# One transfer for the first input tile, norm-weight rows asked first, and a changed order of two vector operations at the beginning of the MLP

## The chip, the cores and the metric

The kernel runs on one core of one Trainium2 chip. Its metric is device time in microseconds (us), taken as the median of several runs. One execution was also profiled, instruction by instruction; all rows shown are from that execution. TensorE is called PE, VectorE DVE, ScalarE ACT, GpSimd POOL and SyncE SP, as in the profile. SP and ACT also issue DMA transfers, and so does POOL.

## The reference

The reference is a trunk of two layers over 512 tokens of width 1024, all in float32. Cut to what matters here, a layer is:

```python
def hybrid_layer(x, ...):
    h = rmsnorm(x, norm_mix)            # x * rsqrt(mean(x^2) + eps) * gain
    z = h @ w_in                        # 1024 -> 4360 columns
    ...                                 # windowed attention, mLSTM, two gates
    x = x + mixed @ w_out
    u = jax.nn.relu(rmsnorm(x, norm_ffn) @ w_ff1)   # 1024 -> 4096
    return x + (u * u) @ w_ff2                      # 4096 -> 1024
```

## The kernel before

**Split products.** Every matrix product is made with float32 precision from two reduced parts of each operand: `high` is the operand rounded to float32r, `low` is the rest. A product is three matmuls, high by high, high by low and low by high (`mm3`, whose matmuls all carry L47, the line of the helper that records the latest PE instruction; PE transposes carry L52). The two parts of an activation are made by `split` (L196, L197, or L199, L200 with a scale), those of a weight by L186, L187 in the mixer and L1268, L1269 in the MLP: ACT makes the high part, and DVE subtracts it to make the low part.

**The norm.** The normalised activations are not formed directly. `Norm.turn(k)` transposes the k-th 128 columns of x (four PE transposes, one per block of 128 tokens, into one PSUM bank) and splits them with the norm gain as a scale per partition; the factor per token is applied later. So a bank with transposed x is read by ACT (high) and then by DVE (low), and it is free for the next transposes when both have read it.

**The start.** x lies in four tiles of 256 tokens by 512 columns. The first 128 columns come by two transfers, 256 tokens each, one issued by SP and one by ACT (`load_x`, L375). ACT then issues `gain0` (L382), the first 128 norm weights as one number to each of 128 partitions, and `grow0` (L383), all norm weights of the mixers as 16 rows of 128. Then come the next 128 columns of x, again by SP and by ACT, and ACT loads its activation table (L387). SP alternates pieces of x with the weight chunks of the first four output blocks (L159). Meanwhile PE multiplies a matrix of ones into a bank called `idle`, transposes the first tile of x, and multiplies ones once more. `turn_first` makes the high part of the first tile in two halves with `gain0` as the scale (ACT, L315) and queues the low part (DVE, L319) behind the split of the first weight chunk (DVE, L171 and L173). The first group of four output blocks runs term by term for k = 0: high weight by high x in four blocks, then low weight by high x, then high weight by low x, four matmuls each. Between the first and the second term PE transposes `grow0` into a spare part of the bank `idle`, DVE copies the result to `gcol` (L134), from which all later gains are taken, and PE transposes x for k = 1.

**The beginning of the MLP.** The MLP uses a fast scheme with half-sized blocks, seven products in place of eight, which needs sums and differences of quarters of x. `turn_whole(k)` for k = 0 to 3 transposes a piece of x into one of the two auxiliary PSUM banks; ACT copies the second token half with the gain (L1366) into a tile called `one`; `norm.turn` splits the whole piece (ACT L199, then DVE L200); and DVE makes the difference of the token halves, with the gain, from the bank and `one` (L1368). The bank thus has four readers. It is called twice after the first half-product and twice after the second, so the third and fourth call reuse the banks of the first and second.

**What sets the order.** A planner lists the instructions of each engine before the run, from its own estimates of durations: of those that it takes to be ready it issues the one with the lowest rank. Inside a `high_priority` block the ranks count from zero at the head of the block, so the place in its block is an instruction's rank against those of other such blocks. `issue_after` forces an order on one engine without a wait. At run time each engine's own list is fixed and executed in order. DMA transfers of SP and ACT are counted on eight completion counters in turn; a ninth transfer waits until the first has landed.

Of the kernel before, what the change touches and what calls it, by code (L numbers as in the profile page):

```python
# [8 lines left out]
F32 = mybir.dt.float32  # L9
# [7 lines left out]
P = 128  # L17
T = 512
NB = T // P
D = 1024  # L20
KT = D // P
# [8 lines left out]
LN_EXP = "natural_log_exp_and_others"  # L30
# [3 lines left out]
def hybrid_kernel(ctx, tc, x, norm_mix, w_in, att_q_norm, att_k_norm, att_sinks, m_gate_bias,  # L34
                  m_head_norm, w_att_branch, w_m_branch, w_out, norm_ffn, w_ff1, w_ff2,
                  rope_cos, rope_sin, out):
    nc = tc.nc
    ve, sc, gp = nc.vector, nc.scalar, nc.gpsimd

    latest = [None]  # L40
# [14 lines left out]
    const = ctx.enter_context(tc.tile_pool(name="const", bufs=1))  # L55
    small = ctx.enter_context(tc.tile_pool(name="small", bufs=3))
# [5 lines left out]
    def nm(s):  # L62
        uid[0] += 1
        return f"{s}_{uid[0]}"
# [33 lines left out]
    def aux(shape=(P, T)):  # L98
        return now["paux"].tile(list(shape), F32, tag="aux", name=nm("aux"))
# [4 lines left out]
    def f32(ap):  # L104
        return ap.bitcast(F32)
# [7 lines left out]
    grow0 = const.tile([16, P], F32, name="grow0")  # L113
# [11 lines left out]
    grow = const.tile([24, P], F32, name="grow")  # L125
    gcol = const.tile([P, 40], F32, name="gcol")

    first_gains = []

    def gains(row, c0, gps=None):  # L130
        n = row.shape[0]
        gps = aux([P, n]) if gps is None else gps
        pe.transpose(gps, row, ident[:n, :n])
        return ve.tensor_copy(gcol[:, c0:c0 + n], gps)  # L134

    def g_mix(l, k):
        return gcol[:, 8 * l + k:8 * l + k + 1]
# [8 lines left out]
    chunks, asked, lead, first_rest = [0], [None], [None], []  # L146

    def chunk(src, behind=()):

        with tc.high_priority():  # L150
            raw = now["wraw"].tile([P, T], F32, tag="w", name=nm("w"))
            off = 0
            for s in src:
                n = s.shape[1]
                if first_loads:

                    n0 = {0: 0, 1: 2}.get(chunks[0], len(first_loads) - 1)
                    with tc.issue_after(first_loads[n0].ins):
                        first_weights.append(nc.sync.dma_start(raw[:, off:off + n], s))  # L159
                    chunks[0] += 1  # L160
                    if chunks[0] == 8:
                        first_loads.clear()
                else:
                    asked[0] = nc.sync.dma_start(raw[:, off:off + n], s)
                off += n
        with tc.high_priority(lead[0]):
            wh = now["wsp"].tile([P, T], F32R, tag="wh", name=nm("wh"))
            wl = now["wsp"].tile([P, T], F32R, tag="wl", name=nm("wl"))
            n = chunks[0] - 1 if first_loads else KT
            if n == 0 and first_rest:  # L170
                high = ve.tensor_copy(wh[:, :off], raw[:, :off])  # L171
                with tc.issue_after(high.ins):
                    low = ve.tensor_tensor(wl[:, :off], raw[:, :off], f32(wh[:, :off]), op=ALU.subtract)  # L173
                with tc.issue_after(low.ins):
                    first_rest.pop()()
                return wh, wl
            with ExitStack() as order:
                for i in behind:
                    order.enter_context(tc.issue_after(i.ins))
                if n == 1:  # L180
                    order.enter_context(tc.issue_after(first_gains[0].ins))
                if n < KT:

                    order.enter_context(tc.issue_after(norm0.hi[max(n - 1, 0)].ins))
                    order.enter_context(tc.issue_after(norm0.lo[max(n - 1, 0)].ins))
                sc.activation(wh[:, :off], raw[:, :off], AF.Copy)  # L186
                ve.tensor_tensor(wl[:, :off], raw[:, :off], f32(wh[:, :off]), op=ALU.subtract)  # L187
        return wh, wl
# [169 lines left out]

    junk = const.tile([P, T], BF16, name="junk")

    xtok = [[const.tile([P, 2, T], F32, name=f"x{t}_{j}") for j in range(2)] for t in range(2)]
    gain0 = small.tile([P, 1], F32, tag="gain0", name=nm("gain0"), bufs=1)
    norm = norm0 = Norm(lambda k: g_mix(0, k) if k else gain0)
    first_loads, first_weights = [], []

    def load_late(k):

        with tc.high_priority(), tc.issue_after(first_weights[-1].ins):
            for t in range(2):
                load_x(k, 2, t, nc.sync)  # L370

    def load_x(k, n, t, by):

        c = (k % 4) * P
        first_loads.append(by.dma_start(  # L375
            xtok[t][k // 4][:, :, c:c + n * P],
            x[0, 2 * t * P:2 * (t + 1) * P, k * P:(k + n) * P].rearrange("(i p) n -> p i n", p=P)))

    with tc.high_priority():
        load_x(0, 1, 0, nc.sync)  # L380
        load_x(0, 1, 1, nc.scalar)
        nc.scalar.dma_start(gain0, norm_mix[0, 0:P].rearrange("(p o) -> p o", o=1))  # L382
        nc.scalar.dma_start(grow0, norm_mix.rearrange("l (k p) -> (l k) p", p=P))  # L383
        load_x(1, 1, 0, nc.sync)
        load_x(1, 1, 1, nc.scalar)
        with tc.issue_after(first_loads[-1].ins):
            sc.preload_act_table_set(LN_EXP)  # L387
        for t in range(2):
            load_x(2, 2, t, nc.sync)

        idle = aux()
        for n in (2, 2, 2):
            pe.matmul(idle[:, :n * P], ones, ones.unsqueeze(1).to_broadcast([P, n, P]), start=True, stop=True)
        with tc.issue_after(latest[0].ins):
            x0 = [aux((P, 2 * P)) for _ in range(2)]
            for b in range(NB):
                pe.transpose(x0[b // 2][:, b % 2 * P:(b % 2 + 1) * P], xtok[b // 2][0][:, b % 2, 0:P], ident)
        with tc.issue_after(latest[0].ins):
            pe.matmul(idle[:, :P], ones, ones, start=True, stop=True)
        norm.turn_first(x0)  # L400
# [838 lines left out]
    def mlp(l, norm, phase):  # L1239
# [117 lines left out]
        def turn_whole(k):  # L1357

            ps = norm.transposes(k)
            if not whole:  # L1360
                whole[:] = [quads.tile([P, 4, H], F32, tag="q5", name=nm("x")),
                            uspl.tile([P, 4, H], F32, tag="uh", name=nm("x"))]
                scratch["b"] = quads.tile([P, 4, H], F32, tag="s", name=nm("x"))
            one = whole[k % 2][:, k, :]
            with tc.high_priority():
                sc.activation(one, ps[:, H:T], AF.Copy, scale=norm.gain(k))  # L1366
                norm.turn(k, ps)
                ve.scalar_tensor_tensor(scratch["b"][:, k, :], ps[:, :H], norm.gain(k), one,  # L1368
                                        op0=ALU.mult, op1=ALU.subtract)

        def x22():
            h22, l22 = [f32(a) for a in quad(1, 1)]
            scratch["a"] = uspl.tile([P, 4, H], F32, tag="ul", name=nm("x"))
            plus(scratch["a"], h22, l22)
# [402 lines left out]
        p = second_slots(0, us[0])  # L1777
        slots = [f0[2], f1[2], f0[1], f0[5], p[1], f0[6], f0[7], f0[4], f0[3],
                 f1[1], p[5], f1[5], p[6], f1[6], p[3], f1[7], p[7], f1[3], p[4], f1[4], p[2]]
        for part in range(1, 4):  # L1780
            p = second_slots(part, us[part])
            if part < 3:
                f = first_slots(part + 1, us[part + 1])[1]
# [34 lines left out]
        def squares():  # L1818
            with tc.issue_after(sums_made[3][0].ins):
                norm.squares(0)  # L1820

        turns = [(1.0 + k // 2, lambda k=k: turn_whole(k)) for k in range(4)]
        x22()
        weave([(1.0, go) for _, go in steps[:10]], turns + [(9.0, squares), (9.0, factor)])
# [8 lines left out]
    def turn_behind(norm, k):  # L1833

        with tc.issue_after(latest[0].ins):
            norm.turn(k)

    def gains_behind():

        with tc.issue_after(latest[0].ins):  # L1840
            first_gains.append(gains(grow0, 0, idle[:, 2 * P:2 * P + 16]))

    late = ([(0.2, gains_behind)] + [(max(0.25, k - 0.85), lambda k=k: turn_behind(norm, k)) for k in range(1, KT)]
            + [(3.0, lambda: load_late(4)), (4.0, lambda: load_late(6))]
            + [(6.5, late_gains)]
            + [(3.0 + 2.2 * j, lambda j=j: norm.squares(j)) for j in range(2)])
    order = None
    for l in range(DEPTH):
        with start if l == 0 else ExitStack() as phase:
            if l > 0:  # L1850
                psum_pools(phase, 3)
            norm = mixer(l, norm, late, order, phase)
        with ExitStack() as phase:
            psum_pools(phase, 2)
            norm = mlp(l, norm, phase)
        late = []
        if norm:
            late = [(0.75, lambda k=k, norm=norm: turn_behind(norm, 6 + k)) for k in range(2)]
            late += [(1.25, lambda norm=norm: norm.squares(1))]
            late += norm.steps(0, 1.75, 0.5, lambda k, norm=norm: turn_behind(norm, k))  # L1860
        order = [4, 5, 6, 7, 0, 1, 2, 3]
# [40 lines left out]
```

## Time and profile before

| | |
|---|---|
| median of 3 runs | 1261.53 us (1261.37 to 1263.22) |
| the profiled execution | 1262.1 us, of which the span is 1260.4 us |
| busy: PE, weight loads, DVE, ACT, POOL | 1254.8, 1100.6, 1029.8, 813.5, 281.1 us |
| first matmul of the program | starts 1.08 us into the span |
| first matmul on x | recorded from 5.73 us |
| transposes of the third `turn_whole` | start at 325.45 us (layer 0), 950.15 us (layer 1) |

The span is the time from the first to the last instruction; what lies around it, 1.7 us here, is launch and end. PE executes in order, and its matmuls overlap, so a row gives the start of the first and the time to the end of the last; the distance between the starts of neighbours is the cost of one. Idle time in brackets names what ended it.

### The profile page before, as it was taken

What the parts mean: (1) busy time and instruction counts of PE and PEld (TensorE: products, weight loads), DVE (VectorE), ACT (ScalarE), POOL (GpSimd) and SP (SyncE); (2) the same over time, 40 slices, a digit from 0 to 9 for tenths busy, and PEclk for the clock granted to TensorE, in tenths of its full rate; (3) what the DMA queues carried; (4) which work ended last, traced back from release to release, by engine and by line L of the source; (5) the groups of instructions that cost most, each with busy time, mean ns of one, the idle gap of its engine ahead of it and who ended that gap; (6) DMA issues with size and microseconds to landing.
All of it is one profiled execution on the core that took longest, in us unless ns stands there. A gap on an engine that the chain in (4) does not pass through costs nothing.

```text
span 1260.4 us, 19852 instructions
## 1 busy us (share of the span) xinstructions
PE 1254.8 (100%) x7178; PEld 1100.6 (87%) x7178; DVE 1029.8 (82%) x1598; ACT 813.5 (65%) x1443; POOL 281.1 (22%) x373
## 2 busy tenths in 40 slices
PE   9999999999999999999999999999999999999998
PEld 7888888888999899999888888888889999999987
DVE  4788997688998887878857989876889988778787
ACT  5578578646685665656554885876467766556563
POOL 4513231021222021131115032310303211311300
PEclk9999999999999999999999999999999999999999
DMA  5424573469799889997224354644778997998943
GB/s 164 118 70 128 134 129 97 130 140 236 156 250 181 234 171 212 234 188 199 35 76 118 88 130 118 118 117 117 157 219 178 239 199 220 172 227 203 200 134 101
DMA packets 145410, 199.68 MB, mean 158 GB/s; under 512 B 10904, under 2 KB 85504, under 8 KB 145312
## 3 DMA queue, kind: packets, MB, share of 16 engines
q0 software_dynamic: 50432, 68.30, 33.8%
q1 hardware_dynamic: 94016, 129.72, 33.1%
q8 instruction: 56, 0.92, 0.3%
q10 hardware_dynamic: 864, 0.40, 0.1%
q14 instruction: 42, 0.34, 0.1%
HBM read 195.24 MB, written 2.10 MB: 157 GB/s over the span
## 4 chain that ended last, share of the span: by engine, by line
PE 98%; DVE 1%; DMA 0%; issue 0%; ACTq 0%; ACT 0%; DVEq 0%
PE mm L47 83%; PE aux L47 12%; PE aux L52 2%; DVE wl L1269 1%; DMA gain<-in_norm_mix_dram 0%; DVE i L200 0%; DVE x L1314 0%; DVE raw L1314 0%; DVE x L1368 0%; ACTq L375 0%; DVE x L1333 0%; ACT i L315 0%; DVEq L200 0%; ACTq L315 0%
## 5 line engine op out<-in xcount | busy, mean ns | idle before, releaser
L1268 ACT ACTIVATE wh<-raw 128x1024 fp32r<-128x1024 f32 x224 | 234.8, 1054 | 152.1 <-PE mm L47 85.1
L1269 DVE TENSOR_TENSOR wl<-raw,wh 128x1024 fp32r<-128x1024 f32 x224 | 271.5, 1221 | 72.2 <-ACT wh L1268 69.4
L47 PE MATMUL mm<-i,wh 128*128 128x256 f32 (+1 forms) x1344 | 330.3, 338 | 0.0
L47 PEld LDWEIGHTS mm<-i,wh 128*128 128x128 f32 x1344 | 225.0, 190 | 20.5
L47 PE MATMUL mm<-i,wl 128*128 128x256 f32 (+1 forms) x672 | 224.4, 334 | 0.0
L47 PE MATMUL mm<-wh,uh 128*128 128x512 f32 (+1 forms) x444 | 173.1, 390 | 0.0
L47 PE MATMUL mm<-wl,uh 128*128 128x512 f32 (+1 forms) x444 | 172.8, 389 | 0.0
L47 PE MATMUL mm<-wh,ul 128*128 128x512 f32 (+1 forms) x444 | 172.3, 388 | 0.0
L1431 POOL DMA_DIRECT2D raw<-in_w_ff_dram x56 | 72.5, 1375 | 343.3 <-DVE wl L1269 91.4
L47 PEld LDWEIGHTS mm<-i,wl 128*128 128x128 f32 x672 | 127.6, 190 | 13.3
L187 DVE TENSOR_TENSOR wl<-w,wh 128x512 fp32r<-128x512 f32 (+1 forms) x143 | 94.4, 665 | 34.0 <-ACT wh L186 31.6
L186 ACT ACTIVATE wh<-w 128x512 fp32r<-128x512 f32 (+1 forms) x143 | 85.0, 601 | 54.4 <-PE mm L47 48.0
L47 PE MATMUL mm<-t,wh 128*128 128x256 f32 x576 | 104.5, 283 | 0.0
L47 PE MATMUL mm<-wh,i 128*128 128x512 f32 (+1 forms) x352 | 98.7, 357 | 0.4 <-ACT i L315 0.4
L47 PEld LDWEIGHTS mm<-wh,ul 128*128 128x128 f32 x444 | 83.4, 188 | 17.4
L47 PEld LDWEIGHTS mm<-wh,uh 128*128 128x128 f32 x444 | 83.5, 188 | 16.1
L47 PEld LDWEIGHTS mm<-wl,uh 128*128 128x128 f32 x444 | 83.5, 188 | 15.7
L47 PEld LDWEIGHTS mm<-t,wh 128*128 128x128 f32 x576 | 90.7, 192 | 1.3
L1683 POOL DMA_DIRECT2D raw<-in_w_ff_dram x40 | 48.2, 1207 | 175.9 <-DVE wl L1269 136.8
L1333 DVE SCALAR_TENSOR_TENSOR x<-mm,ms,x 128x512 f32<-128x512 f32 (+1 forms) x103 | 73.0, 743 | 11.3 <-PE mm L47 11.0
L47 PE MATMUL mm<-t,wl 128*128 128x256 f32 x288 | 81.5, 283 | 0.0
L47 PEld LDWEIGHTS mm<-wh,i 128*128 128x128 f32 x352 | 62.3, 189 | 9.6 <-ACT i L315 0.7
(333 smaller groups left out, 2517.3 us busy)
## 6 DMA issues: line engine op xcount, KB each, us to landing
raw<-in_w_ff_dram SPq DMA_DIRECT2D x144, 512.0 KB, 5.5
raw<-in_w_ff_dram POOLq DMA_DIRECT2D x96, 512.0 KB, 7.9
w<-in_w_in_dram SPq DMA_DIRECT2D x112, 256.0 KB, 2.7
a<-in_w_in_dram POOLq DMA_DIRECT2D x32, 256.0 KB, 5.2
qa<-in_w_out_dram POOLq DMA_DIRECT2D x12, 512.0 KB, 5.9
a<-in_w_in_dram SPq DMA_DIRECT2D x16, 256.0 KB, 4.4
w<-in_w_att_branch_dram SPq DMA_DIRECT2D x16, 256.0 KB, 3.7
w<-in_w_m_branch_dram SPq DMA_DIRECT2D x16, 256.0 KB, 2.9
```

Of the source, the lines that this page charges most:

```text
L47: latest[0] = nc.tensor.matmul(*args, **kw)
L52: latest[0] = nc.tensor.transpose(*args)
L186: sc.activation(wh[:, :off], raw[:, :off], AF.Copy)
L187: ve.tensor_tensor(wl[:, :off], raw[:, :off], f32(wh[:, :off]), op=ALU.subtract)
L1268: last_high[0] = sc.activation(hi, src, AF.Copy)
L1269: last_rest[0] = ve.tensor_tensor(lo, src, f32(hi), op=ALU.subtract)
L1333: ve.scalar_tensor_tensor(xh[:, cc], ps[i][c[0] // H] if halved else ps[i], ms[j][:, b:b + 1], xh[:, cc], op0=ALU.mult, op1=ALU.add)
L1431: return gp.dma_start(to[h], src(h, i, j), accum_op=ALU.add)
L1683: gp.dma_start(to[h], src(h, i, j), accum_op=ALU.add)
```

## The change

Three edits are made together.

1. x lies in two tiles of 512 tokens by 512 columns; the four old tiles are views of them. The first 128 columns of all tokens come by one transfer of 256 KB on SP's queue, and ACT's first transfer is now `grow0`. `gain0` is gone. ACT's table load is placed behind the issue of `grow0`, and ACT's share of the next x columns behind the table load.
2. The transpose of `grow0` and the copy to `gcol` move ahead of the first transposes of x; the split of the first weight chunk is placed behind that copy on DVE, and the first tile's gain is taken from `gcol` like all others.
3. In `turn_whole`, the difference of the token halves is traced before the split of the whole piece.

```diff
@@ chunk
-                    n0 = {0: 0, 1: 2}.get(chunks[0], len(first_loads) - 1)
+                    n0 = {0: 0, 1: 1}.get(chunks[0], len(first_loads) - 1)
...
-                high = ve.tensor_copy(wh[:, :off], raw[:, :off])
+                with tc.issue_after(first_gains.ins):
+                    high = ve.tensor_copy(wh[:, :off], raw[:, :off])
...
-                if n == 1:
-                    order.enter_context(tc.issue_after(first_gains[0].ins))
@@ start
-    xtok = [[const.tile([P, 2, T], F32, name=f"x{t}_{j}") for j in range(2)] for t in range(2)]
-    gain0 = small.tile([P, 1], F32, tag="gain0", name=nm("gain0"), bufs=1)
-    norm = norm0 = Norm(lambda k: g_mix(0, k) if k else gain0)
+    xall = [const.tile([P, NB, T], F32, name=f"x{j}") for j in range(2)]
+    xtok = [[x_[:, 2 * t:2 * t + 2, :] for x_ in xall] for t in range(2)]
+    norm = norm0 = Norm(lambda k: g_mix(0, k))
...
-        load_x(0, 1, 0, nc.sync)
-        load_x(0, 1, 1, nc.scalar)
-        nc.scalar.dma_start(gain0, norm_mix[0, 0:P].rearrange("(p o) -> p o", o=1))
-        nc.scalar.dma_start(grow0, norm_mix.rearrange("l (k p) -> (l k) p", p=P))
+        first_loads.append(nc.sync.dma_start(xall[0][:, :, 0:P], x[0, :, 0:P].rearrange("(i p) n -> p i n", p=P)))
+        asked_rows = nc.scalar.dma_start(grow0, norm_mix.rearrange("l (k p) -> (l k) p", p=P))
+        with tc.issue_after(asked_rows.ins):
+            table = sc.preload_act_table_set(LN_EXP)
         load_x(1, 1, 0, nc.sync)
-        load_x(1, 1, 1, nc.scalar)
-        with tc.issue_after(first_loads[-1].ins):
-            sc.preload_act_table_set(LN_EXP)
+        with tc.issue_after(table.ins):
+            load_x(1, 1, 1, nc.scalar)
...
+        with tc.issue_after(latest[0].ins):
+            first_gains = gains(grow0, 0, idle[:, 2 * P:2 * P + 16])
         with tc.issue_after(latest[0].ins):
             x0 = [aux((P, 2 * P)) for _ in range(2)]
@@ turn_whole
                 sc.activation(one, ps[:, H:T], AF.Copy, scale=norm.gain(k))
-                norm.turn(k, ps)
                 ve.scalar_tensor_tensor(scratch["b"][:, k, :], ps[:, :H], norm.gain(k), one,
                                         op0=ALU.mult, op1=ALU.subtract)
+                norm.turn(k, ps)
@@ end
-    def gains_behind():
-
-        with tc.issue_after(latest[0].ins):
-            first_gains.append(gains(grow0, 0, idle[:, 2 * P:2 * P + 16]))
-
-    late = ([(0.2, gains_behind)] + [(max(0.25, k - 0.85), lambda k=k: turn_behind(norm, k)) for k in range(1, KT)]
+    late = ([(max(0.25, k - 0.85), lambda k=k: turn_behind(norm, k)) for k in range(1, KT)]
```

More of the change, by code (lines that the diff above doesn't have):

```diff
@@ L126, in hybrid_kernel @@
     gcol = const.tile([P, 40], F32, name="gcol")
-    first_gains = []
     def gains(row, c0, gps=None):
```

## The prediction

> **What bounds the kernel now.** I read the page first, then PE's waits, then the timeline around each place where PE waited.
>
> ```profile
> span 1260.4 us, 19852 instructions
> PE 1254.8 (100%) x7178; PEld 1100.6 (87%) x7178; DVE 1029.8 (82%) x1598; ACT 813.5 (65%) x1443; POOL 281.1 (22%) x373
> PE 98%; DVE 1%; DMA 0%; issue 0%; ACTq 0%; ACT 0%; DVEq 0%
> ```
>
> ```profile
> engine line waited for: us in total, times, longest us
> PE aux L47 <- POOL ones L112: 1.1, 1, 1.1
> PE mm L47 <- ACT i L315: 0.4, 1, 0.4
> PE aux L52 <- DVE x L1368: 0.3, 2, 0.2
> ```
>
> PE is busy for 1254.8 of 1260.4 us and makes 98% of the chain that ended last. It waits at only four places in the whole program: once for the matrix of ones, which the change doesn't touch, once at the first matmul on x, and once per layer at the beginning of the MLP. No matmul and no transpose is removed. So a gain can only come from the last three waits, and what PE wins there arrives at the end in full, because behind them PE runs without a gap. A loss can come from anywhere.
>
> **The start.** The chain and the timeline of the first 11 us:
>
> ```profile
> 0.82 0.50 ACTq L375 DMA_DIRECT2D x<-in_x_dram  x1
> ...
> 1.87 0.45 ACTq L383 DMA_DIRECT2D grow<-in_norm_mix_dram  x1
> ...
> 2.35 0.45 ACTq L375 DMA_DIRECT2D x<-in_x_dram  x1
> 2.82 1.28 ACT L387 ACT_TABLE_LOAD   x1 [2.82 <-issue]
> ...
> 3.80 1.06 PE L52 MATMUL aux<-ident,x 128*128 128x128 f32 x4
> 4.65 0.64 PE L47 MATMUL aux<-ones 128*128 128x128 f32 x2
> 4.86 0.43 DVE L171 CAST wh<-w 128x512 fp32r<-128x512 f32 x1 [3.37 <-DMA w<-in_w_in_dram]
> ...
> 5.20 0.84 ACT L315 ACTIVATE i<-aux,gain 128x256 fp32r<-128x256 f32 x2 [1.09 <-DMA gain<-in_norm_mix_dram]
> ...
> 5.73 1.77 PE L47 MATMUL mm<-wh,i 128*128 128x512 f32 x4 [0.44 <-ACT i L315]
> ...
> 7.43 0.23 PE L52 MATMUL aux<-ident,grow 16*128 16x16 f32 x1
> 7.59 0.66 PE L52 MATMUL aux<-ident,x 128*128 128x128 f32 x4
> 7.70 0.17 DVE L134 COPY gcol<-aux 128x16 f32<-128x16 f32 x1 [0.90 <-PE aux L52]
> ...
> 10.41 0.39 PE L47 MATMUL mm<-wh,i 128*128 128x512 f32 x1
> 10.64 0.60 PE L52 MATMUL aux<-ident,x 128*128 128x128 f32 x4
> ```
>
> The transposes of x are done at 4.86 and the first weight's high part at 5.29, yet ACT begins the high part of x at 5.20, because `gain0`, asked at 1.35, lands at 5.11. ACT ends both halves at 6.04. The first matmul reads all 512 columns, so it can't begin before that, whatever its recorded start of 5.73.
>
> *Afterwards.* `grow0` is ACT's first transfer, asked at 0.82. Its landing is not in this trace, so it is bounded by these rows:
>
> ```profile
> x<-in_x_dram ACTq DMA_DIRECT2D x1, 128.0 KB, 2.9
> x<-in_x_dram SPq DMA_DIRECT2D x1, 128.0 KB, 2.7
> ...
> gain<-in_norm_mix_dram ACTq DMA_DIRECT2D x1, 0.5 KB, 3.8
> grow<-in_norm_mix_dram ACTq DMA_DIRECT2D x1, 8.0 KB, 4.2
> ...
> x<-in_x_dram ACTq DMA_DIRECT2D x1, 128.0 KB, 5.3
> ...
> GB/s 0 0 0 0 0 0 36 75 239 347 401 384 252 81 75 164 333 375 362 347 379 394 360 328 362 362 328 324 321 345 362 393 362 355 345 287 341 369 365 379
> ...
> SPq L375 <- DMA x<-in_x_dram: 1.7, 2, 1.0
> ```
>
> Between 2.7 us after the ask (3.52) and 4.2 (5.02, its own row now, but there it stood behind `gain0`). I take 2.9, what ACT's first transfer takes now: 3.72. PE is free for it at 3.80, where the transposes of x start now. It costs PE 0.16 (7.43 to 7.59). The transposes of x then end at 5.02 in place of 4.86; `gcol` is ready 0.44 after the start of its transpose (7.43 to 7.87), at 4.24, long before. The first half of x is transposed at about 4.6, ACT needs 0.47 for each half (half of 0.84 with its overlap), and the second half, ready at 5.02, is scaled by 5.55. The first matmul can start at about 5.55 in place of 6.04: 0.49 us sooner. The weight's high part is ready at 5.29 as now; the copy to `gcol`, behind which it is queued, is over by 4.24. The matmuls on ones still fit in front of 5.55.
>
> x in one transfer of 256 KB: the two halves take 2.7 and 2.9 now, together 256 KB at the same time, so I take 2.9, landing 3.7; bounds 2.7 and 3.5, what the 256 KB weight chunk takes (landing 4.3, which would give back 0.5). The weight chunk lies behind the same bytes as before.
>
> *What 0.49 us sooner is worth.* Four transposes of x take 1.06 us at 3.80 and 0.60 at 10.64: PE runs at about half speed at the beginning. From 6.04 the first four matmuls take until 7.50; less the 0.39 of the last that is a spacing of 0.36, between the 0.23 of later ones (10.41 to 10.64) and twice that, so the step lies among them, near 7 us. If the step moves with the work, the gain is 0.49; if it stays where it is, the 0.49 us are filled at half speed and give 0.25. I take the middle, 0.37. On this the Trainium skill (TensorE: Matmul & The Clock Gate, section What's actually happening) says that the half clock is released after an activity window of about 3.4 us that runs freely, not restarted by the kernel. The two rows of transposes agree with the half speed; that the step doesn't depend on the work, one execution can't show. By that rule the term is 0.25 and the sum below 1.16.
>
> *What leaves the stream behind it.* Now the transpose of `grow0` stands between the first and the second term. The fourth matmul starts at 7.50 less 0.39, 7.11; a transpose of x follows a matmul after 0.23 elsewhere (10.41 to 10.64), so it could start at 7.34, but starts at 7.59: 0.25 us at full speed, gone.
>
> *What must come in time.* With 0.62 us together, the x transposes for k = 1 begin at about 7.0; the third of them reads ACT's piece, which now lands at 2.35 + 5.3 = 7.65. It is asked behind the table load afterwards: at 1.27 if the issue doesn't wait for the load, at 2.6 (1.28 us later) if it does. The row of GB/s (0.3 us each) shows a hole from 3.9 to 4.8, mean 107 against about 360: some 0.23 MB or 0.6 us not moved, at the time when `gain0`'s 128 separate numbers are under way. Without them I put the landing at 7.0, just in time; bounds 4.2 (1.27 + 2.9) and 7.9 (2.6 + 5.3). SP's later asks come sooner, since two transfers fewer stand in front: the 1.7 us it waits for x to land go; that costs PE nothing, the chunks land ahead of use.
>
> **The beginning of the MLP.** The same place of layer 0 on DVE, ACT and PE, and PE's wait in layer 1:
>
> ```profile
> 321.24 1.22 DVE L1314 TENSOR_TENSOR raw<-raw,raw 128x1024 f32<-128x1024 f32 x1
> 322.37 1.41 DVE L200 SCALAR_TENSOR_TENSOR i<-aux,gcol,i 128x512 fp32r<-128x512 f32 x2
> 323.69 1.22 DVE L1269 TENSOR_TENSOR wl<-raw,wh 128x1024 fp32r<-128x1024 f32 x1
> 324.83 0.87 DVE L1368 SCALAR_TENSOR_TENSOR x<-aux,gcol,x 128x256 f32<-128x256 f32 x2
> 325.61 1.22 DVE L1314 TENSOR_TENSOR raw<-raw,raw 128x1024 f32<-128x1024 f32 x1
> ...
> 319.72 0.82 ACT L1366 ACTIVATE x<-aux,gcol 128x256 f32<-128x256 f32 x2
> ...
> 322.46 1.05 ACT L1268 ACTIVATE wh<-raw 128x1024 fp32r<-128x1024 f32 x1
> ...
> 325.00 0.28 PE L47 MATMUL mm<-i,wh 128*128 128x256 f32 x1
> 325.45 1.06 PE L52 MATMUL aux<-ident,x 128*128 128x128 f32 x8 [0.17 <-DVE x L1368]
> ...
> 950.15 1.06 PE L52 MATMUL aux<-ident,x 128*128 128x128 f32 x8 [0.16 <-DVE x L1368]
> ```
>
> DVE is the late engine, without a gap here. The differences (L1368) could go from 320.54, when ACT's copies are done, but they stand behind both low parts (L200) and a weight's low part (L1269). The first is over at 325.31 (324.83 and half of 0.87 with its overlap) and frees the first bank; PE, whose matmuls follow each other by 0.12 here (0.28 less the overlap), was ready at 325.12 and starts at 325.45: 0.33 us lost per layer, twice as much as the bracket says, since the brackets count from the modelled end of the last matmul.
>
> Afterwards the differences rank second in their block and the low parts fourth. No instruction is added or removed. With the spacings of these rows (L1314 1.13, a low part 0.66, a difference 0.39, L1269 1.14): differences from 322.37 to 323.15, low parts to 323.90 and 324.56, weight to 325.69. Both banks are free by 324.56, before 325.12: gain 0.33 per layer, 0.66. The weight's low part ends 0.78 later than now; behind it wait a transfer that reuses the raw tile and a half-product that is more than one half-product ahead (48 matmuls of 0.12, 5.8 us), so this costs nothing; without that lead it would cost the same 0.78. The low parts' first readers are a half-product still further on.
>
> **The sum.** 0.37 + 0.25 + 0.66 = 1.28 us, from 1262.1 for the profiled execution to 1260.8. That execution is 0.6 above the median of the runs, so from the median, 1261.53, to 1260.25; I say 1260.3.
>
> **Rivals.**
>
> *The low parts hold the banks instead.* Ranked fourth, they fall behind the weight's low part, which ranks second and is ready at 323.69. Then DVE runs differences, weight, low parts; the first bank is free at 323.69 + 1.14 + 0.75 = 325.58, 0.27 later than now: 0.54 lost in place of 0.66 gained, 1261.53 - 0.62 + 0.54 = 1261.5. A half form, one low part before the weight, gives 1260.9. For: the rows show that DVE always has other work. Against: at 323.15 the weight isn't ready yet, a low part is.
>
> *The start's gain is held by the second x tile.* If ACT's piece lands at 7.65 to 7.9 as bounded, the third x transpose for k = 1 starts where it does now and the 0.62 is gone: 1260.9. Landing of `grow0` at 5.02 does the same or slightly worse, since PE in order holds the x transposes behind it (the first matmul at 6.6): 1261.2. For: the row of 4.2. Against: that one stood behind 128 numbers.
>
> *Slower.* The low parts fall behind the weight's and also behind the next sum of raw weights (the L1314 at 325.61, rank one). The first bank is then free 1.13 later again, 326.71, and the second at 327.37: PE starts the fourth piece's transposes at 327.5, now about 325.9: 1.6 lost per layer, 3.2, less 0.62: 1264.1. It decides from the point where the planner takes that sum as ready before a low part has been issued. Against: in the present order it was ready only behind five other instructions.
>
> *Nothing changes in the MLP.* The planner may keep its order, if the tile for the differences isn't free earlier: 1260.9.
>
> **Chances and range.** Forecast 0.52 (own range 1259.6 to 1261.0), banks held by low parts 0.15, start held 0.14, nothing in the MLP 0.07, slower 0.05; 0.07 for an order that shifts elsewhere in the program, which can only cost, since PE has no other wait to win. The range 1259.2 to 1262.2 takes all but the last two and the scatter of the runs, 1261.37 to 1263.22. About 0.2%, 2.5 us, is what a measurement of this kernel tells from no change; nearly all cases lie inside. Faster than 1259.0 would need more than all waits together: 0.04. Slower: 0.06. Same: 0.90.
>
> **What would show it.** Right: the first matmul on x ready by about 5.6 without a wait for a gain's DMA; x transposes for k = 1 straight behind the first term; no hole in the GB/s near 4 us; DVE's L1368 in front of L200 at both MLPs; PE's wait for L1368 gone and none for L200. Wrong: PE waiting for `grow0` near 4 us, for x near 7, or for L200 near 325, or a new wait anywhere.

## The result: slower by 0.45%, and the profile after

The changed kernel takes 1267.43 us (median of 6 runs, 1266.26 to 1268.98) against 1261.53 for before (now also 6 runs, 1261.37 to 1263.22). The ratio on record is 1.0045, 95% interval 1.0034 to 1.0056; the two medians alone give 1.0047. The forecast was 1260.3, with a range of 1259.2 to 1262.2, and no change. The profiled execution took 1266.41 us, 4.3 more than the profiled one of before; it is among the two shortest of the six, and why the others are longer is told in the last section.

The page of after: span, busy times, and (from the chain of waits) the shares of the lines.

```profile
span 1264.7 us, 19840 instructions
PE 1256.8 (99%) x7178; PEld 1100.4 (87%) x7178; DVE 1029.8 (81%) x1598; ACT 813.8 (64%) x1443; POOL 282.8 (22%) x373
by line: PE mm L47 81.9%; PE aux L47 12.6%; PE aux L52 2.4%; ACT wh L1266 0.5%; DVE wl L1267 0.4%; DVE raw L1312 0.3%; DVE t L1267 0.2%; DVE ul L1267 0.2%; ACT u L1560 0.2%; ACT uh L1266 0.2%; ACT t L1266 0.2%; ACT u L1541 0.2%; ACT u L1559
```

PE still has the same 7178 instructions, but its part of the chain has gone from 98% to 96.9%; ACT and DVE now hold places in it. PE's waits in after say where (us in total, times, longest):

```profile
PE mm L47 <- ACT i L196: 2.1, 2, 1.1
...
PE mm L47 <- DVE i L197: 0.6, 2, 0.3
PE mm L47 <- DVE ul L1267: 0.4, 2, 0.2
PE mm L47 <- DVE t L1267: 0.4, 2, 0.2
```

The waits for the first gain and for the differences (named L315 and L1368 in before) are gone from this list, as forecast. Four new ones stand there, each once per layer. Line numbers have moved by two or three: L196 and L197 are now the scaled split's high and low part (L199, L200), L1364 is ACT's copy (L1366), L1365 the difference (L1368), L1266 and L1267 the high and low part of the MLP's weights (L1268, L1269), L1312 a sum of raw weights (L1314), L1541 ACT's evacuation of a product.

The start in after's timeline, and, from the DMA view of its first 12 us, the GB/s (0.3 us each) and ACT's part of x (KB, us from the ask to the landing):

```profile
1.31 1.28 ACT L380 ACT_TABLE_LOAD   x1 [1.31 <-PEq L1881]
1.34 0.48 ACTq L372 DMA_DIRECT2D x<-in_x_dram  x1
3.94 0.28 PE L52 MATMUL aux<-ident,grow 16*128 16x16 f32 x1
4.15 1.11 PE L52 MATMUL aux<-ident,x 128*128 128x128 f32 x4
...
4.88 0.90 ACT L312 ACTIVATE i<-aux,gcol 128x256 fp32r<-128x256 f32 x2 [2.28 <-PE aux L52]
...
5.63 1.19 PE L47 MATMUL mm<-wh,i 128*128 128x512 f32 x4
6.66 0.60 PE L52 MATMUL aux<-ident,x 128*128 128x128 f32 x4
7.01 1.17 PE L47 MATMUL mm<-wl,i 128*128 128x512 f32 x4
```

```profile
GB/s 0 0 0 0 0 0 104 155 184 311 331 340 271 321 336 377 389 341 253 259 338 372 372 318 352 369 352 345 382 386 382 403 389 379 369 382 372 379 365 396
...
x<-in_x_dram ACTq DMA_DIRECT2D x1, 128.0 KB, 4.0
```

This part does what was forecast: no wait for `grow0` or x, no hole in the GB/s, the transposes for k = 1 straight behind the first term. The second term (`wl`) starts at 7.01 in place of 8.00. In this execution the start has won 1.0 us, and the end has come 4.3 us later all the same.

The beginning of the MLP in layer 0, ACT, then DVE, then PE:

```profile
318.78 0.82 ACT L1364 ACTIVATE x<-aux,gcol 128x256 f32<-128x256 f32 x2
321.02 0.60 ACT L1541 ACTIVATE u<-mm 128x512 f32<-128x512 f32 x1 [1.42 <-PE mm L47]
...
322.94 1.27 ACT L196 ACTIVATE i<-aux,gcol 128x512 fp32r<-128x512 f32 x2
...
329.47 0.70 ACT L196 ACTIVATE i<-aux,gcol 128x512 fp32r<-128x512 f32 x1
...
321.41 0.87 DVE L1365 SCALAR_TENSOR_TENSOR x<-aux,gcol,x 128x256 f32<-128x256 f32 x2
...
323.74 0.74 DVE L197 SCALAR_TENSOR_TENSOR i<-aux,gcol,i 128x512 fp32r<-128x512 f32 x1
...
326.66 0.48 DVE L1365 SCALAR_TENSOR_TENSOR x<-aux,gcol,x 128x256 f32<-128x256 f32 x1
327.06 0.74 DVE L197 SCALAR_TENSOR_TENSOR i<-aux,gcol,i 128x512 fp32r<-128x512 f32 x1
...
324.54 0.65 PE L52 MATMUL aux<-ident,x 128*128 128x128 f32 x4
...
327.95 0.63 PE L52 MATMUL aux<-ident,x 128*128 128x128 f32 x4
...
328.89 0.28 PE L47 MATMUL mm<-i,wl 128*128 128x256 f32 x1
330.22 0.50 PE L47 MATMUL mm<-i,wh 128*128 128x256 f32 x2 [1.05 <-ACT i L196]
331.01 0.39 PE L47 MATMUL mm<-i,wh 128*128 128x256 f32 x1 [0.28 <-DVE i L197]
```

and what ACT and DVE did in the place of it before:

```profile
320.43 1.27 ACT L199 ACTIVATE i<-aux,gcol 128x512 fp32r<-128x512 f32 x2
...
326.49 0.68 ACT L199 ACTIVATE i<-aux,gcol 128x512 fp32r<-128x512 f32 x1
...
327.88 1.40 DVE L200 SCALAR_TENSOR_TENSOR i<-aux,gcol,i 128x512 fp32r<-128x512 f32 x2
```

Before, ACT made the two high parts at 320.43, right behind its two copies (319.72). In after the copies begin at 318.78 and the high parts at 322.94, although ACT sat idle for 1.42 us in between. The low parts on DVE come later with them (323.74 and 327.06 in place of 322.37), the second bank is free only at 327.8 (327.06 + 0.74), and the fourth piece is transposed at 327.95; before, both pieces were transposed in one go at 325.45. The third piece's high part, at 326.49 before, comes at 329.47. PE has run out of other work at 329.01 (328.89 and a spacing of 0.12) and stands until it is there. The brackets count from a matmul's modelled end, so they say less than is lost: from 329.01 to 330.22 are 1.21 us; two matmuls from 330.22 would let the next start at 330.46, which starts at 331.01, 0.55 lost. The waits for DVE's `t` and `ul` behind it stand only in kernels that make the whole exchange, and in none of the others, so I take them for a consequence of the same delay.

### The profile page after: what moved, and what is told of

Same layout as the page of the kernel before. It is cut to its first block, busy times and chain, and to the rows that moved or that the text cites. A ratio compares the mean times of both kernels' runs of the same rounds, so it can differ in the third digit from the quotient of the medians.

```text
span 1264.7 us, 19840 instructions
## 1 busy us (share of the span) xinstructions
PE 1256.8 (99%) x7178; PEld 1100.4 (87%) x7178; DVE 1029.8 (81%) x1598; ACT 813.8 (64%) x1443; POOL 282.8 (22%) x373
## 4 chain that ended last, share of the span: by engine, by line
PE 97%; ACT 1%; DVE 1%; issue 0%; POOL 0%; DVEq 0%; ACTq 0%; POOLq 0%
PE mm L47 82%; PE aux L47 13%; PE aux L52 2%; ACT wh L1266 1%; DVE wl L1267 0%; DVE raw L1312 0%; DVE ul L1267 0%; DVE t L1267 0%; ACT u L1560 0%; ACT uh L1266 0%; ACT t L1266 0%; ACT u L1541 0%; ACT u L1559 0%; ACT i L196 0%; DVE x L1365 0%
## 5 line engine op out<-in xcount | busy, mean ns | idle before, releaser
L1266 ACT ACTIVATE wh<-raw 128x1024 fp32r<-128x1024 f32 x224 | 234.7, 1055 | 160.8 <-PE mm L47 80.6
L1267 DVE TENSOR_TENSOR wl<-raw,wh 128x1024 fp32r<-128x1024 f32 x224 | 271.5, 1221 | 75.2 <-ACT wh L1266 74.1
```

Of the source, the lines that this page charges most:

```text
L1266: last_high[0] = sc.activation(hi, src, AF.Copy)
L1267: last_rest[0] = ve.tensor_tensor(lo, src, f32(hi), op=ALU.subtract)
```

## The experiments

A first reading of these rows was one of **rank**: inside its block the high part has fallen from second to third place, so the planner lists weights' parts and evacuations in front of it on ACT. The first four runs were made under that theory; the last two set it against another. All kernels of the table but `turn_only` have the change's new start. Each group of runs was timed together with before, which gave 1261.73 us beside the first four, 1261.66 beside `pair1` and `pair2` (and `tiny_load` and `two_x`, further down) and 1261.56 beside the last two. The last column adds up the waits that the profile lists at the MLP; a delay of 0.3 us can be missing from that list, as is shown below.

| run | MLP's order of a piece | median, us | ratio to before (95%) | PE's waits in the MLP, us |
|---|---|---|---|---|
| `start_only` | old | 1261.27 | 0.9997 (0.9988 to 1.0006) | none |
| `turn_only` (old start) | exchanged | 1267.29 | 1.0046 (1.0034 to 1.0059) | 3.5 |
| `high_first` | copy, high, difference, low | 1261.12 | 0.9995 (0.9986 to 1.0003) | none |
| `own_block` | exchanged, split in a block of its own | 1269.66 | 1.0060 (1.0047 to 1.0072) | 4.3 |
| `pair1` | exchanged for pieces 1 and 2 | 1262.80 | 1.0010 (1.0001 to 1.0019) | 1.0 |
| `pair2` | exchanged for pieces 3 and 4 | 1265.11 | 1.0027 (1.0016 to 1.0037) | 2.3 |
| `rank_only` | ranks exchanged, readers in the old order | 1261.23 | 1.0000 (0.9991 to 1.0009) | none |
| `bank_only` | readers exchanged, old ranks | 1266.89 | 1.0043 (1.0030 to 1.0056) | 3.2 |

### `start_only` and `turn_only`: each part alone

`start_only` is after without the exchange, `turn_only` is before with nothing but the exchange:

```diff
                 sc.activation(one, ps[:, H:T], AF.Copy, scale=norm.gain(k))
-                norm.turn(k, ps)
                 ve.scalar_tensor_tensor(scratch["b"][:, k, :], ps[:, :H], norm.gain(k), one,
                                         op0=ALU.mult, op1=ALU.subtract)
+                norm.turn(k, ps)
```

> The changed kernel with the old order of turn_whole: only the start edits. Theory A (the start gains 1.0 us in the trace, shift of PE by -1.01 us at 10 us, and the whole loss comes from the MLP's beginning) : 1261.5 - 1.0 = 1260.5 us, PE waits only for the ones and twice 0.16 us for the differences of the MLP, as before. Rival C (the start edits, through the merged x tiles or the earlier transfers, also carry a part of the loss): 1263 us or more, with a wait that the old kernel does not have.

> The old kernel with only the two operations of turn_whole exchanged. Theory A (each layer loses 2.8 us of PE there, shift from -1.0 to +1.8 and from +1.8 to +4.7 us): 1261.5 + 5.7 = 1267.2 us, waits for the high part of 1.05 us and for the low part of 0.28 us in each layer. Rival C: under 1263 us.

PE's waits in `turn_only`:

```profile
PE mm L47 <- ACT i L199: 2.1, 2, 1.0
...
PE mm L47 <- DVE i L200: 0.6, 2, 0.3
...
```

The exchange alone gives 5.6 us (1267.29 less 1261.73) and the same four waits with the same sizes as after. The start alone gives 1261.27, 0.46 less than before beside it, which the interval doesn't tell from nothing, and 0.8 more than the 1260.5 that was expected. Its only listed wait is the one for the ones, but the delay in front of the third piece's transposes is still there: they start at 325.22, where the matmul before them, at 324.79 with its spacing of 0.12, would have let them start at 324.91. So the whole loss is the exchange, and the start, for all its edits, costs nothing.

### `high_first` and `own_block`: where the high part stands

`high_first` traces the difference between the high and the low part; `own_block` keeps the exchange and puts the split into a `high_priority` block of its own, so that the high part ranks first in it:

```diff
+            with tc.high_priority():
                 norm.turn(k, ps)
```

> The changed kernel, with turn_whole in the order copy of the second half, high part, difference, low part: the high part has its old rank, the difference still stands in front of the low part. Theory A (the loss is the high parts' fall behind other work of ACT, which PE then waits for): the wait of 1.05 us for the high part is gone, the old wait of 0.16 us for the difference too; at most 0.3 us per layer is left for a low part: 1259.8 to 1260.5 us. Rival B (DVE is full there, and any order with the differences ahead makes the low parts late enough to stall PE): half of the loss or more stays, 1263 us or more, with waits for the low part of over 1 us per layer.

> The changed kernel, with the split of turn_whole in a high-priority block of its own, so that its high part ranks first and its low part second again, behind the difference in program order. On ACT's list the high parts of the third and fourth call still stand behind the copies of both, and the fourth behind a weight, a result and the first difference's high part. Theory A: PE still waits for a high part, less than 1.05 us, and the loss per layer is between 0.5 and 2.8 us: 1261.5 to 1266 us. Rival B (the low parts decide): the same as the changed kernel, about 1266.5 us, for the second of the first two low parts stands behind the same sum of raw weights, the fourth behind the same difference.

With the high part in its old place nothing is lost (1261.12), although the low part has fallen one place; the gain that was expected, to 1260.5 or less, didn't come either. That nothing is lost fits the rank theory. `own_block` doesn't fit: the high part now has the best rank there is, and the kernel is the slowest of all, above both expectations. Part of that is a half clock that its waits bring on, some 1.4 us in layer 0 (18 matmuls in place of 31 in a stretch of 3.41 us, last section); less such a stretch per layer, as an estimate, `own_block` would be near the change, so it shows that a better rank doesn't help rather than that it hurts. Its longest wait is for `t`, whose high part ACT makes behind a late high part of x:

```profile
PE mm L47 <- ACT t L1266: 3.3, 2, 1.7
...
```

### `pair1` and `pair2`: which pieces

```diff
+                if k > 1:            # pair1; pair2 has k < 2
+                    norm.turn(k, ps)
                 ve.scalar_tensor_tensor(...)
-                norm.turn(k, ps)
+                if not (k > 1):
+                    norm.turn(k, ps)
```

> All of the change but one half of it: the exchanged order (copy, difference, high part, low part) only for the first two pieces of x at the MLP's beginning, the old order (copy, high, low, difference) for the third and fourth. Theory C1, the loss comes from the first two pieces' own place: their high parts stand on ACT behind weights' parts, free their banks later, and so the third and fourth pieces are transposed and scaled late: then nearly all the loss is here, 1265 to 1267.5 us, with PE waiting for ACT's i (L196) for about 1 us per layer near 329. Theory C2, the loss comes from the third and fourth pieces' own place, since PE reads their parts within about 1 us of their being made: then 1261 to 1261.8 us here, with no wait for i.

> The counterpart: the old order for the first two pieces, the exchanged order for the third and fourth only. Theory C1: the first two are on time and free their banks as before, so 1261 to 1262 us and no wait for ACT's i. Theory C2: the third and fourth high parts fall behind a weight's part and behind the first t's high part on ACT (about 1 us each) and PE waits for i: 1264 to 1267 us. Both together, each for its part: pair1 and pair2 lose about half each, some 1264.

`pair1` is 1.1 us slower than the before beside it and `pair2` 3.5. Both have the new start; against `start_only`, 0.5 under its before, they cost 1.6 and 3.9, together 5.5, where the whole exchange cost 5.6. Neither of the two theories, C1 and C2, holds alone: each pair costs something by itself, the third and fourth piece over twice as much, and the two add up.

What told more than the times is a row of `pair2`'s timeline (ACT, then DVE):

```profile
325.65 0.91 ACT L1364 ACTIVATE x<-aux,gcol 128x256 f32<-128x256 f32 x2 [0.26 <-PE aux L52]
327.93 0.69 ACT L196 ACTIVATE i<-aux,gcol 128x512 fp32r<-128x512 f32 x1 [1.36 <-DVE x L1367]
...
327.42 0.87 DVE L1367 SCALAR_TENSOR_TENSOR x<-aux,gcol,x 128x256 f32<-128x256 f32 x2
```

Both copies are done at 326.56. The third piece's high part is ACT's next instruction, with nothing in front of it, and it stands for 1.36 us until DVE has made a difference. It needs no number of that difference; it reads the same PSUM bank. That is no matter of rank. The recorded instructions say the same, since each carries the semaphores that it waits for. In before, none of ACT's four high parts of a layer waits for one. In after the first and the third wait for semaphore 101, which DVE's differences count up; the second and the fourth stand behind an instruction of ACT that has waited for it.

### `rank_only` and `bank_only`: rank against bank

A second theory follows: in a kernel that this planner lists, the readers of a bank on two engines take turns in the order in which the program asks for them, and the planner puts a wait at each handover. Before, a piece's turns were ACT, ACT, DVE, DVE (copy, high, low, difference), one handover. In the change they are ACT, DVE, ACT, DVE, three handovers, each with the other engine's queue in front of it. The two runs separate the order in the program from the rank, which is set by hand:

```diff
 # rank_only: asked for in the order copy, high, difference, low
...                                                 # the difference is now `halves`, asked for inside the split
-                norm.turn(k, ps)
+                norm.turn(k, ps, halves, ranks=(2, 1, 3))   # ranks of high, difference, low
 # bank_only: asked for in the order copy, difference, high, low
+                tc.cur_priority = 3                         # the difference ranks last
                 ve.scalar_tensor_tensor(...)
-                norm.turn(k, ps)
+                norm.turn(k, ps, ranks=(1, 2))              # ranks of high, low
```

> The change with its ranks but not its order of readers: the difference ranks before the high part (copy 0, difference 1, high part 2, low part 3, as in the change), but the program asks for the high part before the difference, so that both of ACT's reads of a PSUM bank come before both of DVE's. Theory R (rank): the high part loses its place on ACT because its rank fell from 1 to 2, behind weights' parts; then the loss is here: 1265 to 1267.5 us, with PE waiting about 1 us per layer for ACT's i near 329. Theory B (bank): ACT and DVE never read one bank at the same time, readers take turns in the order of the program, and in the change ACT's high part so got a wait for DVE's difference, which itself waits for ACT's copy; then nothing is lost here: 1260.7 to 1261.6 us, the differences still in front of the low parts on DVE, and no wait for i or for the difference on PE.

> The counterpart: the change's order of readers (copy, difference, high part, low part) with the old ranks (copy 0, high part 1, low part 2, difference 3). Theory R: the high part stands in its old place on ACT, 1260.7 to 1261.6 us. Theory B: the high part still waits for DVE's difference, which now ranks last, so as slow as the change or slower: 1265.5 to 1269 us, PE waiting about 1 us per layer for ACT's i.

`rank_only` loses nothing, `bank_only` nearly all of it: 5.3 us (1266.89 less 1261.56). Both came as the theory of the bank had it (B in these two expectations); the rank theory has fallen. The recorded waits go with it: in `rank_only` none of the four high parts of a layer waits for a semaphore, in `bank_only` three of the four wait for the one of DVE. `bank_only`'s longest wait, and ACT and DVE of `rank_only` at the first two pieces:

```profile
PE mm L47 <- ACT i L198: 1.8, 2, 0.9
...
```

```profile
319.31 0.82 ACT L1371 ACTIVATE x<-aux,gcol 128x256 f32<-128x256 f32 x2
320.02 1.27 ACT L198 ACTIVATE i<-aux,gcol 128x512 fp32r<-128x512 f32 x2
...
321.94 0.87 DVE L1372 SCALAR_TENSOR_TENSOR x<-aux,gcol,x 128x256 f32<-128x256 f32 x2
322.72 0.74 DVE L204 SCALAR_TENSOR_TENSOR i<-aux,gcol,i 128x512 fp32r<-128x512 f32 x1
```

Here are the differences in front of the low parts, just as the change wanted it, and the high parts right behind the copies.

On this the Trainium skill (PSUM — Partial Sum Buffer, section PSUM bank collisions raise a hardware error) says that no two of TensorE, ScalarE and VectorE may access one bank in the same partitions at once, two reads included, and that software has to keep them apart. The rows agree in that the turns are taken; what the chip would do without them no run here shows, since the wait alone was not taken away.

### `tiny_load` and `two_x`: two steps of the start

Both have the old order at the MLP, like `start_only`. `tiny_load` adds the load of 128 separate numbers that the change took away, which nothing reads here; `two_x` asks for x's first columns by two transfers, ACT's behind `grow0`.

```diff
 # tiny_load
+            asked_rows = nc.scalar.dma_start(gain0, norm_mix[0, 0:P].rearrange("(p o) -> p o", o=1))
 # two_x
...
-        first_loads.append(nc.sync.dma_start(xall[0][:, :, 0:P], ...))
+        load_x(0, 1, 0, nc.sync)
...
+            load_x(0, 1, 1, nc.scalar)
```

> The start of the change with the old order at the MLP, and in addition the load that the change took away (128 separate numbers of 4 bytes, here read by nobody), asked behind the norm weights' rows on ACT's queue. If those separate numbers made the hole in the transferred GB/s near 3.9 to 4.8 us, it is there again (a slice below 120 GB/s between 3.6 and 5), and ACT's second x tile lands at 6.5 to 7.7 in place of 5.3; the time stays within 0.5 us of 1261.3. If the hole was only a pause between what had been asked early and what was asked behind it, there is none here either (no slice below 150) and the tile lands at about 5.4 to 5.8 (one more issue of 0.5 us in front of it).

> The start of the change with the old order at the MLP, but x's first columns by two transfers as before, SP's half first on its queue, ACT's half behind the norm weights' rows. If the single transfer is what counts at the start, ACT's half, asked 0.45 us later, lands at 4.1 to 4.3 in place of 3.75, and the first matmul on x is 0.2 to 0.5 us later than with one transfer: 1261.3 to 1261.8 us. If the two halves share the same bytes per us anyway, they land at 3.7 to 3.9 and the time is 1261.3, as with one transfer.

From the DMA view of `tiny_load`'s first 12 us, and PE's waits:

```profile
GB/s 0 0 0 0 0 0 87 131 231 350 364 340 182 128 74 87 138 285 290 336 335 364 386 386 360 393 362 365 369 376 341 362 365 355 369 355 365 348 369 348
...
x<-in_x_dram ACTq DMA_DIRECT2D x1, 128.0 KB, 6.4
```

```profile
PE aux L52 <- DMA x<-in_x_dram: 0.9, 2, 0.7
```

The hole is back: 74 and 87 GB/s from 4.2 to 4.8 us, where after has 336 and 377. ACT's x tile takes 6.4 us in place of 4.0 and lands near 8.3, later than the 6.5 to 7.7 that was expected, and PE waits 0.9 us for x. The median is 1262.02 (1261.16 to 1263.08; ratio to before 1.0003, 0.9994 to 1.0012). That is 0.75 above `start_only`, a little more than the 0.5 that was expected; since the two were timed beside different runs of before and neither interval leaves out 1, it doesn't show a loss.

`two_x`'s PE waits for the second half of x:

```profile
5.51 0.44 PE L52 MATMUL aux<-ident,x 128*128 128x128 f32 x2 [0.96 <-DMA x<-in_x_dram]
```

ACT's half lands at about 5.5, later than both expectations had it, and the second product term still starts at 7.44, among those of the kernels with one transfer (6.80 to 7.71, below). The time, 1262.18 (1260.84 to 1263.56; ratio 1.0004, 0.9995 to 1.0013), lies above what either case was expected to give, 1261.3 to 1261.8, but its runs scatter by 2.7 us and don't tell it from one transfer.

## Why the prediction was wrong, step by step

**The step that failed** is in the part on the beginning of the MLP: "Afterwards the differences rank second in their block and the low parts fourth. No instruction is added or removed." What is added is a wait: ACT's high part waits for DVE's difference, because both read one bank, and the sum put that at nothing; it didn't look at the high part at all. The sum took the order of DVE alone ("differences from 322.37 to 323.15, low parts to 323.90 and 324.56"), as if the low parts' input were there. In after the differences do go first, at 321.41, but the high parts can only follow when those are done, at 322.28, when ACT has been given other work, and are made at 322.94; the first low part comes at 323.74 and the second at 327.06. Gain of 0.66 forecast, loss of 5.6 found (`turn_only`).

**The cover was worked out for the wrong pieces.** "The low parts' first readers are a half-product still further on" speaks of the first two pieces, and no wait for their parts is listed. The third and fourth call, whose pieces PE needs next, were never worked out. In after PE has no other work from 329.01 and stands for the third piece's high part; by `pair2` it is in this pair that most of the loss arises. How late these parts could have come at no cost no run shows; in `rank_only` the last low part ends at 329.6 and PE goes on.

**The slower rival** had the place nearly right: it let the second low part fall behind a weight's and behind the next raw sum, and the fourth piece's transposes start at 327.5; in after they start at 327.95. Its price, 1.6 us per layer for late transposes, was not what happened: PE passed over that with other products and stood later, for the high part. At 0.05 it was held for unlikely because "in the present order it was ready only behind five other instructions", which looked at the present order and not at the readiness that the exchange changes.

**The MLP's gain was mis-sized too.** In `rank_only` the differences come first and nothing is lost, yet it is no faster than `start_only` (1261.23 and 1261.27), whose order is the old one. The sum set 0.33 us per layer against it, the distance from 325.12 to 325.45. PE's rows of `rank_only` show where that went:

```profile
323.15 0.40 PE L47 MATMUL mm<-i,wh 128*128 128x256 f32 x2
323.61 0.63 PE L52 MATMUL aux<-ident,x 128*128 128x128 f32 x4
...
325.40 0.63 PE L52 MATMUL aux<-ident,x 128*128 128x128 f32 x4
```

The planner puts the third piece's transposes earlier, and there they wait for the first low part, which is done at 323.46 (322.72 + 0.74): the two matmuls from 323.15 would have let them start at 323.39, so 0.22 us stand there, and the list of waits leaves them out. The fourth piece's transposes don't wait (the matmul before them starts at 325.27). The transposes come in two groups, and the first matmul behind a group costs 0.20 in place of 0.12 each time (323.99 to 324.19, 325.79 to 325.99; in before once, 326.27 to 326.47). So the wait has moved from the difference to a low part, a small form of the rival in which the low parts hold the banks, and next to nothing of the 0.33 is left.

**The start was right in its steps; its size is not shown.** In after, `grow0` was there when PE was free for it (3.94; 3.80 forecast), no x was waited for, and the transpose of `grow0` left the stream. Not every execution with this start is so smooth: `pair2` and `bank_only` list 0.4 and 0.5 us for the first high part, and `pair1` 0.7 for the first weight's and 0.2 for x, a small form of the rival that the second x tile holds the start. The table load didn't hold ACT's next issue: asked at 1.34 with the load running from 1.31 to 2.59. The first piece's high part was ready at 5.78 (4.88 + 0.90) in place of 5.55 (5.49 by the sum's own terms, 5.02 and 0.47): PE's transposes of x began 0.19 later than forecast, at 4.15 in place of 3.96, and took 1.11 in place of 1.06. The size can't be had from one pair of executions. The second term starts at 8.00 in before and at 7.55 in `turn_only`, which have the same start; at 7.01, 7.71, 7.29, 7.29, 7.10, 7.51, 7.20 and 6.80 in after, `start_only`, `high_first`, `rank_only`, `bank_only`, `pair1`, `pair2` and `own_block`, which share the new one. The means are 7.78 (of only two) and 7.24: 0.54 us, where the sum had 0.37 + 0.25 = 0.62. That the two are so near is in part luck, since each start scatters as much. In the medians it is 0.3 to 0.6, which no interval here separates from nothing.

The rows of that list with the old start (before, `turn_only`):

```profile
8.00 1.18 PE L47 MATMUL mm<-wl,i 128*128 128x512 f32 x4
```

```profile
7.55 1.17 PE L47 MATMUL mm<-wl,i 128*128 128x512 f32 x4
```

The old start differs by 0.45 us between its two executions and the new one by 0.91 among its eight. One reason is the half speed at the beginning, which ends sooner or later: the four transposes of x start at 4.15 in both after and `pair1` and take 1.11 us in the one and 0.66 in the other. That is not all, for `pair1`, which is at full speed so early, reaches the second term only at 7.51, behind its waits for the weight and for x:

```profile
4.15 0.66 PE L52 MATMUL aux<-ident,x 128*128 128x128 f32 x4
...
5.75 1.17 PE L47 MATMUL mm<-wh,i 128*128 128x512 f32 x4 [0.71 <-DVE wh L170]
7.13 0.63 PE L52 MATMUL aux<-ident,x 128*128 128x128 f32 x4 [0.21 <-DMA x<-in_x_dram]
```

The rule of the Trainium skill that the prediction weighed (TensorE: Matmul & The Clock Gate, section What's actually happening), a window that runs freely, fits the two durations at 4.15. For the middle between 0.25 and 0.49 that the prediction took, no run here gives a reason.

No version tried beats both kernels: `high_first`, `rank_only` and `start_only` are 0.3 to 0.6 us under the before beside them, and all three intervals hold 1.

## What to carry to other kernels

With a planner like this one, when two operations on different engines read one PSUM bank, their order in the program is an order of turns. Before exchanging two such operations, write down the readers of the bank by engine and count the handovers: here readers of one engine side by side cost nothing in either order of DVE's two, and alternating ones cost over 5 us. An edit that adds and removes no instruction can still add a wait; look for the instruction that is pushed back, not only for the one that is brought forward.

## What the runs showed of the hardware beside this

A stretch with little matmul work can cost the next stretch at half clock. `own_block`'s mean granted clock is 0.997. Its timeline has a gap of 1.65 us in front of the matmul at 330.88; busy time by stretches of 3.41 us there (columns: stretch, its length, busy us and instructions of PE, PEld, DVE, ACT and POOL, then PE's granted clock, DMA share and GB/s):

```profile
329.27:332.68 3.41, 1.42 (x7) 1.02 (x8) 3.29 (x4) 2.63 (x5) 0.00 (x0) 1.00 1.21 193
332.68:336.09 3.41, 3.41 (x18) 3.41 (x17) 0.07 (x1) 0.00 (x0) 0.00 (x0) 0.50 0.21 32
336.09:339.50 3.41, 3.41 (x31) 3.41 (x30) 1.34 (x3) 1.79 (x2) 0.00 (x0) 1.00 0.02 5
```

In the first stretch PE was busy for 1.42 of 3.41 us; the second ran at 0.50 all through, with 18 matmuls where the third has 31, and then the clock was full again. Layer 1 does the same at 960.73 after a stretch with 1.65 us. The Trainium skill (TensorE: Matmul & The Clock Gate, section What's actually happening) has the clock fall after an idle window of about 3.4 us; here windows in which PE was busy for 42% and 48% were enough. `bank_only` has a window with 65%, and the clock stayed full behind it:

```profile
328.79:332.20 3.41, 2.22 (x17) 1.81 (x15) 2.83 (x4) 3.41 (x7) 0.00 (x0) 1.00 1.23 193
```

Where between 48% and 65% the limit lies, and whether the share is what counts, these runs don't show. A stretch of 3.41 us at half clock takes about 0.0013 off a mean over 1266 us, and after's own runs fit that: the two at a mean clock of 1.000 took 1266.26 and 1266.41, three at 0.999 took 1267.35 to 1267.88, one at 0.997 took 1268.98. So about 1.1 us of the 5.9 between the medians would be not the waits but the clock that they sometimes cost; that is read off the mean clocks, since none of the four longer runs has a trace.
